# Retention in a two-layer backbone: the seven products of a head's v and g in another order, with their sums of weights built another way

## The chip, the cores and the metric

The kernel runs on one core of a Trainium2 chip. Times are device microseconds (us) of that core. The kernel before ran three times, 1942.5 to 1948.24 us with a median of 1943.03; its profiled execution took 1941.29 us, of which the span from the first to the last instruction is 1939.5. The engines: TensorE (PE, matmuls; PEld is its loading of weights), VectorE (DVE), ScalarE (ACT), GpSimd (POOL) and SyncE (SP). DMA transfers are issued from SP's and POOL's queues.

## The reference, cut to what matters

The model has two layers, on 512 latent and 256 context tokens of width 1024. Layer 0 is attention with spatial gating, layer 1 is retention, and each has a feed-forward block behind it. The change lies in retention, with 8 heads, keys of width 128 and values of width 256:

```
q, k, v, g = jnp.split(h_lat @ w_in, splits, axis=-1)
...
kc, vc = jnp.split(h_ctx @ w_in[:, RET_QK_WIDTH:2 * RET_QK_WIDTH + RET_V_WIDTH], [RET_QK_WIDTH], axis=-1)
...
for d in range(2):
    lg = log_decay[d].astype(jnp.float32)
    rev = (lambda a: a[:, ::-1]) if d == 1 else (lambda a: a)
    s_ctx = retention_final_state(rev(kc), rev(vc), lg)
    outs_lat.append(rev(retention_chunked(rev(q), rev(k), rev(v), lg, s_ctx)))
...
    s = jnp.einsum('bhqd,bhkd->bhqk', qf, kf) * decay_intra
    o = jnp.einsum('bhqk,bhkv->bhqv', s, vf) + jnp.einsum('bhqd,bhdv->bhqv', qf * decay_q, S)
    S = S * decay_chunk + jnp.einsum('bhkd,bhkv->bhdv', kf * decay_k, vf)
...
on = ((o - mu) * lax.rsqrt(var + EPS)).reshape(B, N, RET_V_WIDTH) * gn_g.astype(jnp.float32)
return (jax.nn.silu(g) * on.astype(g.dtype)) @ w_out
```

## The kernel before

Every operand of a matmul is kept as a high and a low part, so a product is three matmuls (`mm3`, L94 to L96; L93 where a sum goes on in an open bank). `split` makes the parts: a copy on ACT (L68) for the high one, a subtraction on DVE (L69) for the low one. A block of weights is loaded raw into one of three buffers (tag `raw`) and split into one of three slots (`slot`), taken in turn.

The kernel is written against a tile scheduler. The code gives an order of emission and named tiles with tags and buffer counts; the scheduler places the instructions on each engine, where they then run strictly in that order, and adds waits where a buffer or a value isn't ready. PSUM has banks by tag: "A" four, "B" two, "C" two.

Retention runs head by head. Head 0 uses plain products and makes, once, sums of the token blocks (`h_sums`). In heads 1 to 7 the projection of the 512 latent tokens to v and g (512 columns a head) is a two-by-two scheme with seven products in place of eight. Each is `product`: 24 matmuls of 128x256, of a block (or sum of blocks) of the tokens with a block (or sum of blocks) of the weights. The blocks of weights are called 11, 12, 21 and 22, and four of the seven operands are sums: t1 = 11+12, t2 = 11+12+22, t3 = 12+22, t4 = 11+12+21+22, as far as signs are folded into the stored weights. The sums are made by DMAs that add into a tile in SBUF (`add`, issued on POOL's queue, 512 KB each).

In the kernel before, one tile (`rwr`) is loaded with 11 and grows to t1, t2 and t4; another (`rwt3`) is loaded with 12 and grows to t3. The products go in the order 11, t1, t2, 21, t3, 22, t4. X, Y and Z are their banks; the sum in X runs over 11, t2, t3 and t4 and is read out between. v and g of the first 256 tokens and the rest are taken from these banks, by copies and subtractions. `nat` is the context's v, in two halves (tile `rn`), which use blocks 11 and 21.

Around the products of head h stand: `rk` and `rq` (keys and queries, 24 matmuls of 128x512 each), the transposes `rt` of head h-1's output and their copies `gt` (`gated`), the transposes `kn` of the keys and their weighted copies `kd` (`k_nat`), eight pieces `wr` of the output projection of head h-1 (`out_steps`, tokens 0 to 3, halves 0 and 1; copies `ypr` on ACT into two buffers, then an adding DMA into the result `yr`, issued on POOL), the scores `rs`, the products `ro` of scores and v (`within`), the states `stc` and `stl` (`states`), whose splits `st` go through `sc` and `cm`, the products `rx` of queries and states (`across`), the context's key `rkc` (`k_ctx`), and the norm on DVE. `bg` steps a background task, the conditioning of a later block: loads `ar`, accumulations `acc`, a few small matmuls `ac`. The output weights of head h, two blocks `rwo` with splits `uwh` and `uwl`, are loaded toward the end of head h and used in head h+1.

In the names of tiles the first digit is the head: `rwt23h` is the high part of t2 in head 3, `rwo31r` the second raw block of output weights of head 3, `wr210` the piece of head 2's output for token block 1, half 0.

Of the kernel before, what the change touches and what calls it, by code (L numbers as in the profile page):

```python
# [8 lines left out]
F32 = mybir.dt.float32  # L9
# [4 lines left out]
ALU = mybir.AluOpType  # L14
AX = mybir.AxisListType

P = 128
D = 1024
# [22 lines left out]
class Trunk:  # L41
# [873 lines left out]
    def retention(self, y, final, gates):  # L915
        S, V, T, G, a = self.S, self.V, self.T, self.G, self.a
        KS = float(np.float32(P) ** np.float32(-0.5))
        with ExitStack() as ctx:
            rp = self.phase(ctx, "retp", 0)
# [132 lines left out]
            def vg_tiles(h):  # L1052
                hd[h]["v"] = [rp.tile([P, 6, 256], F32R, name=f"rv{i}{h}", tag=f"rv{i}", bufs=1) for i in range(2)]
                hd[h]["g"] = rp.tile([P, 4, 256], F32, name=f"rg{h}", tag="rg", bufs=1)

            def score(h, c):
# [162 lines left out]
            def vg_units(h):  # L1219

                d = hd[h]
                u = d["u"] = {}
                src = {"11": vg(h, 0, 0), "12": vg(h, 16, 0), "21": vg(h, 0, 1), "22": vg(h, 16, 1)}
                raws = {}

                def add(t, n):
                    G.dma_start(t, src[n], accum_op=ALU.add)  # L1227

                def raw(n, b):
                    raws[n] = self.bp.tile([P, 1024], F32, name=f"rw{n}{h}r", tag="raw", bufs=3)  # L1230
                    self.load(raws[n], src[b])
# [10 lines left out]
                def b11():  # L1242
                    make("b11", raws["r"])
                    add(raws["r"], "12")

                def t1():
                    make("t1", raws["r"])
                    add(raws["r"], "22")
                    raw("b21", "21")
# [7 lines left out]
                def b21():  # L1257
                    make("b21", raws["b21"])
                    raw("b22", "22")

                return [load, b11, t1, t2, b21] + [
                    lambda n=n: make(n, raws["r" if n == "t4" else n]) for n in ("t3", "b22", "t4")
                ]

            def product(ps, b, w, onto=False):
                for t in range(2):
# [6 lines left out]
            def products(h):  # L1273

                d = hd[h]
                u, v, g = d["u"], d["v"], d["g"]
# [3 lines left out]
                product(X, blk[0, 0], u["b11"])  # L1280
                c11 = self.t2k(f"c11{h}", shape=(P, 2, 256))
                S.copy(c11, X)
                nat(h, [u["b11"], None], 2, "v", range(0, 4))
                yield
                Y = bank("y")
                product(Y, blk["s", 1], u["t1"])
                S.copy(g[:, hi], Y)
# [3 lines left out]
                yield  # L1291
                Z = bank("z")
                product(Z, blk[0, 1], u["b21"])
# [3 lines left out]
                nat(h, [None, u["b21"]], 2, "v", range(4, 8))  # L1297
                yield
                product(X, blk["s", 3], u["t3"], True)
                V.tensor_tensor(out=g[:, hi], in0=g[:, hi], in1=X, op=ALU.subtract)  # L1300
                S.activation(g[:, hi], g[:, hi], AF.Silu)
                yield
                product(Y, blk["s", 4], u["b22"], True)
# [3 lines left out]
                product(X, blk[1, 1], u["t4"], True)  # L1307
                self.split(v[0][:, hi], v[1][:, hi], X)
                yield

            def ahead(h):

                make = vg_units(h)
                make.pop(0)()
                wq = qk(h, 0, "q")
                make.pop(0)()
                return wq, make

            for h in range(8):
                vg_tiles(h)  # L1320
                if h == 0:
                    two = lambda o, n, d0, d1: [
                        w8(self.unit(vg(h, o, i), f"rw{n}{h}{i}", d)) for i, d in enumerate((d0, d1))
                    ]
# [11 lines left out]
                    for half in range(2):  # L1336
# [6 lines left out]
                        for n, f in enumerate(steps):  # L1343
# [29 lines left out]
                    continue  # L1373
                psk = self.ps(f"rk{h}", "A")
# [6 lines left out]
                self.proj_t(psq, wq, 0)  # L1381
                make.pop(0)()
                q_lat(h, psq)
                self.bg()
                f = gated(h - 1)
# [3 lines left out]
                p = products(h)  # L1389
                for n in range(8):  # L1390
                    if make and n > 0:
                        make.pop(0)()
                    next(p, None)
                    o()
                    if n < 2:
                        o()
                    if n == 1:
                        score(h, 0)
                    if n in (1, 3, 4, 5):
                        self.bg()  # L1400
                    if n == 5:
                        within(h, 0)
                        score(h, 1)
                if h < 7:
                    wk = qk(h + 1, 8, "k")
                    k_ctx(h + 1, wk)
                else:
# [5 lines left out]
                    g = rp.tile([P, D], F32, name="g3", tag="s4h", bufs=1)  # L1413
                    self.load(g, gates[0])
                    gates[0] = g
                states(h)
                across(h, 0)
                across(h, 1)
                within(h, 1)
                across(h, 2)  # L1420
                across(h, 3)
                if h < 7:
                    wq, make = ahead(h + 1)
                norm(h)
            self.out_last(o6, lambda: (gated(7), w_out(7)), y, toks, EARLY, final, "r")

# [516 lines left out]
```

## Time and profile before

| what | value |
|---|---|
| median of three runs | 1943.03 us |
| profiled execution / its span | 1941.29 / 1939.5 us |
| granted TensorE clock, mean | 0.976 |
| stage of retention's heads | from about 975 to 1545 us |
| head 3 (1195.3 to 1266.0): length, PE busy | 70.70, 64.11 us |
| head 7 (from 1481.8): longest wait of PE | 2.1 us, `rx` for `st` |
| POOL's adds `rwr`, issue to landing, median | 5.7 us |
| POOL's `yr`, issue to landing, median | 5.6 us |

The page gives the busy time of each engine; a windows view cuts a stretch of time out and gives the same for it, with the granted clock and the share of time that the DMA engines were busy. The waits view names what PE waited for, with the total, the number and the longest. In a timeline row stand the start, the duration, the engine, the line of the code and the operation; the bracket at its end gives how long the engine stood idle before it, and what released it. An issue of a DMA is a row of SPq or POOL; its landing shows as the releaser of the instruction that used the data.

### The profile page before, as it was taken

To read this page: it belongs to the slowest core of one execution; us is meant where nothing else is said; L and a number is where in the kernel's file an instruction comes from. 1 tells how busy PE (TensorE), PEld (TensorE's weight loads), DVE (VectorE), ACT (ScalarE), POOL (GpSimd) and SP (SyncE) were. 2 spreads that over 40 slices of the span, in tenths; PEclk is the share of its full clock that TensorE was granted. 3 is DMA by queue.
4 is the path that set the end of the run, shared out by engine and by line. 5 is a ranking of instruction groups with operands and counts; after the bars stand their busy time and mean duration, and the time that the engine had idled before them with its cause. 6 is when DMAs were issued, how large, how long until landed. Compare 5 with 4: busy or idle time off the path is not lost. (4 is left out here: it accounts for less than half of the span.)

```text
span 1939.5 us, 28779 instructions
## 1 busy us (share of the span) xinstructions
PE 1799.0 (93%) x10760; PEld 1586.0 (82%) x10760; DVE 1432.5 (74%) x2370; ACT 1080.3 (56%) x1947; POOL 417.3 (22%) x540
## 2 busy tenths in 40 slices
PE   8998989979999999999988999899999879999998
PEld 4886767669889899998787978888888769988997
DVE  4844788689887778777788657566555779989887
ACT  6523545666655466555565545445444467667763
POOL 1102213120122222221143132232132010222221
PEclk9999999989999999999999999999999989999999
DMA  8323333142667778776534656855844433877772
GB/s 286 120 86 104 93 112 93 44 142 91 185 158 154 174 147 181 151 158 159 206 125 107 192 108 160 201 115 129 197 91 89 158 111 121 216 201 185 176 168 98
DMA packets 95188, 280.72 MB, mean 145 GB/s; under 512 B 12092, under 2 KB 13628, under 8 KB 95048
## 3 DMA queue, kind: packets, MB, share of 16 engines
q1 hardware_dynamic: 58856, 202.81, 32.5%
q0 software_dynamic: 36192, 76.08, 23.5%
q8 instruction: 84, 1.38, 0.3%
q14 instruction: 56, 0.46, 0.1%
HBM read 209.12 MB, written 52.95 MB: 135 GB/s over the span
## 5 line engine op out<-in xcount | busy, mean ns | idle before, releaser
L216 DVE SCALAR_TENSOR_TENSOR acc<-ar,cs,acc 128x512 f32<-128x512 f32 x256 | 193.5, 774 | 60.8 <-DMA ar<-in_adaw 36.8
L1671 POOL DMA_DIRECT2D yf<-yp x64 | 55.2, 864 | 259.6 <-ACT yp L1667 160.4
L1522 ACT ACTIVATE cv<-pre,cw 128x770 f32<-128x770 f32 (+1 forms) x88 | 80.9, 923 | 27.3 <-DVE pre L1515 26.0
L1523 DVE SCALAR_TENSOR_TENSOR cv<-pre,cw,cv 128x769 f32<-128x769 f32 (+1 forms) x88 | 77.3, 882 | 8.4 <-ACT cv L1522 8.4
L1510 ACT ACTIVATE pre<-px 128x256 f32<-128x256 f32 (+2 forms) x160 | 54.2, 365 | 46.6 <-PE px L93 37.3
L1667 ACT COPY yp<-wf 128x512 f32<-128x512 f32 x118 | 67.8, 576 | 19.3 <-PE wf L96 19.1
L1526 DVE SCALAR_TENSOR_TENSOR cv<-pre,cw,cv 128x769 f32<-128x769 f32 (+1 forms) x88 | 77.3, 882 | 0.7
L1671 POOL DMA_DIRECT2D yd<-ypg x48 | 41.8, 889 | 133.8 <-ACT ypg L1667 132.3
L1671 POOL DMA_DIRECT2D yd<-yp x48 | 42.4, 898 | 127.1 <-ACT yp L1667 126.9
L1179 POOL DMA_DIRECT2D yr<-ypr x40 | 34.6, 865 | 110.2 <-ACT ypr L1175 110.2
L68 ACT ACTIVATE g<-cv 128x770 fp32r<-128x770 f32 (+1 forms) x44 | 32.5, 738 | 31.1 <-DVE cv L1530 31.0
L94 PE MATMUL wr<-uwh,gt 128*128 128x512 f32 x96 | 38.8, 404 | 9.3 <-ACT gt L1137 9.3
L93 PE MATMUL px<-hs,wd 128*128 128x384 f32 x240 | 45.4, 337 | 0.0
L1175 ACT COPY ypr<-wr 128x512 f32<-128x512 f32 x48 | 27.8, 579 | 30.5 <-DMA yr<-ypr 19.7
L1515 DVE TENSOR_TENSOR pre<-pre,pz 128x256 f32<-128x256 f32 (+1 forms) x60 | 20.8, 373 | 32.4 <-PE pz L96 32.4
L93 PEld LDWEIGHTS px<-hs,wd 128*128 128x128 f32 x240 | 42.3, 188 | 1.8 <-DVE pre L1515 0.3
L1510 ACT ACTIVATE pre<-py 128x384 f32<-128x384 f32 (+1 forms) x40 | 17.4, 436 | 45.2 <-DVE cv L1526 27.1
L1227 POOL DMA_DIRECT2D rwr<-in_ret_vg x21 | 18.8, 897 | 108.1 <-DVE rwb111l L69 14.7
L69 DVE TENSOR_TENSOR g<-cv,g 128x770 fp32r<-128x770 f32 (+1 forms) x44 | 36.2, 822 | 7.3 <-ACT g L68 7.2
L1530 DVE TENSOR_TENSOR cv<-cv 128x770 f32<-128x770 f32 (+1 forms) x44 | 36.2, 824 | 4.7 <-ACT cv L1529 3.5
L1529 ACT ACTIVATE cv<-cv 128x770 f32<-128x770 f32 (+1 forms) x44 | 32.7, 743 | 10.7 <-DVE cv L1526 10.6
L95 PE MATMUL wr<-uwl,gt 128*128 128x512 f32 x96 | 38.4, 400 | 0.0
(3424 smaller groups left out, 7237.9 us busy)
## 6 DMA issues: line engine op xcount, KB each, us to landing
ar<-in_adaw SPq DMA_DIRECT2D x96, 512.0 KB
yf<-yp POOLq DMA_DIRECT2D x64, 256.0 KB, 4.6
yd<-yp POOLq DMA_DIRECT2D x54, 256.0 KB, 5.4
yd<-ypg POOLq DMA_DIRECT2D x54, 256.0 KB, 5.1
yr<-ypr POOLq DMA_DIRECT2D x48, 256.0 KB, 5.6
rwr<-in_ret_vg POOLq DMA_DIRECT2D x21, 512.0 KB, 5.7
fin<-xd SPq DMA_DIRECT2D x10, 512.0 KB
xd<-xd SPq DMA_DIRECT2D x8, 512.0 KB
```

The costliest lines, as they stand in the source:

```text
L69: self.V.tensor_tensor(out=lo, in0=src, in1=hi.bitcast(F32), op=ALU.subtract)
L93: mm = lambda *p, **k: self.nc.tensor.matmul(*p, skip_group_check=True, **k)
L94: mm(out, lhs[0], rhs[0], start=first, stop=False)
L95: mm(out, lhs[0], rhs[1], start=False, stop=False)
L216: V.scalar_tensor_tensor(out=acc[s], in0=raw[:, kk * 512 : kk * 512 + 512], scalar=self.cs[:, 8 * s + k : 8 * s + k + 1], in1=acc[s], op0= ...
L1510: S.activation(pre[:, i, c : c + w], ps[:, b : b + w], AF.Copy, scale=scale)
L1522: S.activation(d, s, AF.Identity, scale=w1, bias=b)
L1523: V.scalar_tensor_tensor(out=d[:, 1:W], in0=s[:, 0 : W - 1], scalar=w0, in1=d[:, 1:W], op0=ALU.mult, op1=ALU.add)
L1526: V.scalar_tensor_tensor(out=d[:, 0 : W - 1], in0=s[:, 1:W], scalar=w2, in1=d[:, 0 : W - 1], op0=ALU.mult, op1=ALU.add)
L1530: V.tensor_tensor(out=cv[:, 0], in0=cv[:, 0], in1=cv[:, 1], op=ALU.mult)
L1667: S.copy(v, ps)
L1671: G.dma_start((yd[t] if first else y[t])[:, o], v, accum_op=ALU.add)
```

## The change

The products of heads 1 to 7 go in the order 11, t2, t3, t4, 21, t1, 22. The sum in X thus runs through without other products between, and t1 (after the first `within` and the second score) and 22 (after the states, ahead of the second `within`) stand among the state's steps. The order of emission is written out in place of the loop.

The sums: one tile is loaded with 12 and gets 22 in the head in front (t3), then 11 (t2), then 21 (t4), each after the split of the sum before. t1 is made in another tile, 11 plus 12, in the memory of the v tile (tag `rv1`), which is allocated afterwards. 11, 21 and 22 are also loaded raw as operands of their own. A head has five loads and four adds for them, where it had four and four; each moves 512 KB. Blocks that were called `rwb11`, `rwb21` and `rwb22` when split are now called `rw11`, `rw21`, `rw22`.

The context's bank `rn` is moved from tag "A" to "C" for heads above 0. The background step ahead of `h_sums` in head 0 is taken out, so that each later step of that task comes earlier or later by one in its list. `across` now follows the second `within` for all four token blocks, and `k_ctx` of the next head comes behind it. Some lines of the diff are left out here:

```diff
-                    hd[h]["rn", tp] = self.ps(f"rn{h}{tp}{dst}", "A", (P, 2, 256))
+                    hd[h]["rn", tp] = self.ps(f"rn{h}{tp}{dst}", "C" if h and tp == 2 else "A", (P, 2, 256))
...
-                def load():
+                def start():
                     raws["r"] = rp.tile([P, 1024], F32, name=f"rwr{h}", tag="vgr", bufs=1)
-                    self.load(raws["r"], src["11"])
...
+                    self.load(raws["r"], src["12"])
+                    add("r", "22")
+
+                def first():
+                    plain("11")
+                    raws["t1"] = rp.tile([P, 1536], F32, name=f"rwt1{h}r", tag="rv1", bufs=1)[:, :1024]
+                    self.load(raws["t1"], src["11"])
+
+                def t3():
+                    make("t3", raws["r"])
+                    add("r", "11")
 
                 def t2():
-                    raw("t3", "12")
                     make("t2", raws["r"])
-                    add(raws["r"], "21")
-                    add(raws["t3"], "22")
...
+                    add("r", "21")
+
+                def t4():
+                    make("t4", raws["r"])
+                    add("t1", "12")
...
-                    self.bg(2)
                     sums = h_sums()
...
+                make = hd[h]["make"]
                 psk = self.ps(f"rk{h}", "A")
                 self.proj_t(psk, wk, 0)
                 k_lat(h, psk)
                 psq = self.ps(f"rq{h}", "A")
                 decay(h)
+                make["t3"]()
+                self.proj_t(psq, wq, 0)
+                q_lat(h, psq)
                 if h < 7:
                     wo = w_out(h - 1)
...
+                make["t2"]()
+                f = gated(h - 1)
+                g_tile(h)
+                p = products(h)
+                next(p)
                 self.bg()
...
                 k_nat(h)
+                make["t4"]()
                 pieces = out_steps(h - 1, f, wo) if h < 7 else []
                 o = lambda: pieces and pieces.pop(0)()
...
+                o()
+                o()
+                next(p)
+                o()
+                score(h, 0)
+                make["21"]()
+                next(p)
+                self.bg()
+                o()
+                make["t1"]()
+                v_tiles(h)
+                next(p)
+                if h < 7:
+                    hd[h + 1]["make"] = vg_units(h + 1)
+                    hd[h + 1]["make"]["start"]()
+                o()
+                make["22"]()
+                next(p)
+                self.bg(2)
+                o()
+                next(p)
+                o()
+                o()
                 if h < 7:
                     wk = qk(h + 1, 8, "k")
...
+                within(h, 0)
+                self.bg()
+                score(h, 1)
+                next(p)
+                states(h)
+                next(p)
...
                 within(h, 1)
-                across(h, 2)
-                across(h, 3)
+                for t in range(4):
+                    across(h, t)
                 if h < 7:
-                    wq, make = ahead(h + 1)
+                    k_ctx(h + 1, wk)
+                    wq = ahead(h + 1)
                 norm(h)
```

The scheduler decides what this makes of the order on each engine. On ACT, near the start of head 3, before, from the copies for the queries' rope on (the bracket names what a row waits for: DMASW is a transfer of POOL's queue, DMAHW one of SP's):

```order
L1137 ACTIVATE gt02_11249<-rt20_11251,gng_9014 128x512 [waits PE_49,Activation_49]
L1137 ACTIVATE gt02_11249<-rt21_11258,gng_9014 128x512 [waits PE_49]
L988 ACTIVATE kd03_11265<-kn30_11267,e03_11185 128x256 [waits PE_49,Activation_49]
L988 ACTIVATE kd03_11265<-kn31_11275,e03_11185 128x256 [waits PE_49]
L68 ACTIVATE rwt23h_11355<-rwr3_11106 128x1024 [waits DMASW1_49]
L68 ACTIVATE rq03_11234<-m1q3_11236 128x512 [waits DVE_49]
```

and after the change:

```order
L68 ACTIVATE rwt23h_11240<-rwr3_10794 128x1024 [waits DMASW1_49]
L1139 ACTIVATE gt02_11245<-rt20_11247,gng_9014 128x512 [waits PE_49,Activation_49]
L1139 ACTIVATE gt02_11245<-rt21_11254,gng_9014 128x512 [waits PE_49]
L68 ACTIVATE rq03_11217<-m1q3_11219 128x512 [waits DVE_49]
L1291 COPY c113_11287<-rx3_11262 128x512 [waits PE_49,Pool_49]
L988 ACTIVATE kd03_11318<-kn30_11320,e03_11182 128x256 [waits PE_49]
L988 ACTIVATE kd03_11318<-kn31_11328,e03_11182 128x256 [waits PE_49]
L68 ACTIVATE rwt43h_11336<-rwr3_10794 128x1024 [waits DMASW2_49]
L988 ACTIVATE kd03_11318<-kn30_11320,e13_11184 128x256 [waits DVE_49]
L988 ACTIVATE kd03_11318<-kn31_11328,e13_11184 128x256 [waits DVE_49]
L1177 COPY ypr_9969<-wr200_11341 128x512 [waits DMASW6_49,PE_49]
L1177 COPY ypr_9969<-wr201_11350 128x512 [waits DMASW7_49,PE_49]
```

The split of t2, which waits for an adding transfer, has moved ahead of both `gt`, and the split of t4, which waits for the next one, ahead of the first two `ypr`.

On ACT at the end of head 3, after the change, from the split of the first block of output weights on:

```order
L68 ACTIVATE uwh3_11921<-rwo30r_11923 128x1024 [waits DMAHW3_49]
L68 ACTIVATE rwq4h_11800<-rwq4r_11798 128x1024 [waits DMAHW1_49,PE_49]
L1314 ACT_TABLE_LOAD
L1314 ACTIVATE rg3_11261<-rg3_11261 128x512 [waits DVE_49]
L68 ACTIVATE st03_11696<-stc3_11670 128x2x256 [waits PE_49]
L68 ACTIVATE uwh4_11927<-rwo31r_11929 128x1024 [waits DMAHW4_49]
L1013 COPY sc3_11701<-stc3_11670 128x512 [waits DVE_49]
L68 ACTIVATE rw114h_11806<-rwb114r_11804 128x1024 [waits DMAHW2_49,PE_49]
L1082 COPY of3_11610<-ro31_11733 128x512 [waits PE_49]
L68 ACTIVATE st03_11696<-cm3_11698 128x512 [waits DVE_49]
```

Before, both splits of output weights stood some rows ahead of the state's, with `rwq4h`, a `silu` and others between; now the second stands between the state's first split and the copy `sc`.

The queue of SP issues the loads. Before, around the output weights of head 3:

```order
L54 DMA rwk4r_11689<-in_ret_qk 128x1024 [waits DMAHW3_49,DVE_49]
L54 DMA rwq4r_11799<-in_ret_qk 128x1024 [waits DMAHW4_49,DVE_49]
L54 DMA rwo30r_11884<-in_ret_out 128x1024 [waits DMAHW5_49,DVE_49]
L54 DMA rwr4_11797<-in_ret_vg 128x1024 [waits DMAHW1_49,DMASW2_49,DVE_49]
L54 DMA rwo31r_11890<-in_ret_out 128x1024 [waits DMAHW6_49,DVE_49]
```

and after the change:

```order
L54 DMA rwo30r_11923<-in_ret_out 128x1024 [waits DMAHW6_49,DVE_49]
L54 DMA rwo31r_11929<-in_ret_out 128x1024 [waits DMAHW3_49,DVE_49]
L54 DMA ar171_12007<-in_adaw 128x1024 [waits DMAHW1_49,DVE_49]
L54 DMA rwb214r_12100<-in_ret_vg 128x1024 [waits DMAHW4_49,DVE_49]
L54 DMA rwt14r_11810<-in_ret_vg 128x1024 [waits DMAHW7_49,DMASW0_49,PE_49]
```

The two loads of output weights now stand directly behind each other. The wait for DVE of `rwo30r` is for the low part of `rwk4`, and that of `rwo31r` for the low part of the block `rwo30r` itself, since both go through the three raw buffers.

More of the change, by code (lines that the diff above doesn't have):

```diff
@@ L1224, in vg_units, with add @@
                 raws = {}
[L1226 to L1231, printed above, removed]
+                def add(n, b):
+                    G.dma_start(raws[n], src[b], accum_op=ALU.add)
                 def make(n, src):
@@ L1275, in products @@
                 d = hd[h]
[L1276 removed]
+                u, g = d["u"], d["g"]
                 lo, hi = slice(0, 2), slice(2, 4)
@@ L1279, in products @@
                 X = bank("x")
-                product(X, blk[0, 0], u["b11"])
+                product(X, blk[0, 0], u["11"])
                 c11 = self.t2k(f"c11{h}", shape=(P, 2, 256))
                 S.copy(c11, X)
[L1283 to L1287, printed above, removed]
+                nat(h, [u["11"], None], 2, "v", range(0, 4))
                 yield
@@ L1291, in products @@
                 yield
+                product(X, blk["s", 3], u["t3"], True)
+                S.copy(g[:, hi], X)
+                yield
+                product(X, blk[1, 1], u["t4"], True)
+                v = d["v"]
+                self.split(v[0][:, hi], v[1][:, hi], X)
+                yield
                 Z = bank("z")
-                product(Z, blk[0, 1], u["b21"])
+                product(Z, blk[0, 1], u["21"])
                 V.tensor_tensor(out=c11, in0=c11, in1=Z, op=ALU.add)
@@ L1296, in products @@
                 yield
-                nat(h, [None, u["b21"]], 2, "v", range(4, 8))
+                nat(h, [None, u["21"]], 2, "v", range(4, 8))
                 yield
-                product(X, blk["s", 3], u["t3"], True)
-                V.tensor_tensor(out=g[:, hi], in0=g[:, hi], in1=X, op=ALU.subtract)
+                Y = bank("y")
+                product(Y, blk["s", 1], u["t1"])
+                V.tensor_tensor(out=g[:, hi], in0=Y, in1=g[:, hi], op=ALU.subtract)
                 S.activation(g[:, hi], g[:, hi], AF.Silu)
                 yield
-                product(Y, blk["s", 4], u["b22"], True)
+                product(Y, blk["s", 4], u["22"], True)
                 V.tensor_tensor(out=g[:, lo], in0=Y, in1=g[:, lo], op=ALU.subtract)
@@ L1412, in retention @@
                         self.load(y[t], yd[t])
[L1413 to L1418, printed above, removed]
+                    gg = rp.tile([P, D], F32, name="g3", tag="s4h", bufs=1)
+                    self.load(gg, gates[0])
+                    gates[0] = gg
                 within(h, 1)
-                across(h, 2)
-                across(h, 3)
+                for t in range(4):
+                    across(h, t)
                 if h < 7:
-                    wq, make = ahead(h + 1)
+                    k_ctx(h + 1, wk)
+                    wq = ahead(h + 1)
                 norm(h)
```

67 lines of the change are left out of this document (24 added, 43 removed).

## The prediction, made before the changed kernel was run

> **What bounds the kernel now.** The page comes first, with the waits of TensorE (PE) in the stage of the change, heads 1 to 7.
>
> ```profile
> span 1939.5 us, 28779 instructions
> PE 1799.0 (93%) x10760; PEld 1586.0 (82%) x10760; DVE 1432.5 (74%) x2370; ACT 1080.3 (56%) x1947; POOL 417.3 (22%) x540
> PE rx L94 <- ACT st L68: 16.0, 7, 2.7
> PE rs L94 <- ACT ypr L1175: 12.0, 5, 3.0
> PE wr L94 <- ACT gt L1137: 9.3, 6, 2.2
> ```
>
> PE is the bound, and only its idle time and its clock can change, since the change moves matmuls and drops none. Three waits make 37.3 us over the stage, about 6 us a head: `rx` (the across products) waits for the state's split, `rs` (scores) stands behind output pieces that wait for ScalarE's (ACT) copies `ypr`, and the first output piece waits for the gated output `gt`. If a product stood before each, that would be the most the change could save.
>
> Next, a head is cut out of the windows. I begin one where PE ends `rk`, which frees a weight slot and so starts ACT's next split (for head 3 the 1195.32 row below); call that instant K.
>
> ```profile
> 1056.60:1126.10 69.50, 65.07 (x425) 58.89 (x425) 45.69 (x73) 34.79 (x52) 17.30 (x27) 0.98 0.63 173
> 1126.10:1195.30 69.20, 63.73 (x425) 57.68 (x424) 43.89 (x73) 34.79 (x52) 19.46 (x24) 1.00 0.67 160
> 1195.30:1266.00 70.70, 64.11 (x429) 57.93 (x428) 43.88 (x75) 35.22 (x53) 19.10 (x23) 1.00 0.65 149
> ...
> 1409.60:1481.80 72.20, 65.74 (x430) 59.20 (x429) 36.28 (x63) 33.64 (x51) 18.52 (x22) 0.98 0.53 103
> ```
>
> Columns: length, busy time of PE, PEld, DVE, ACT and POOL, granted clock, DMA share, GB/s. The six heads between 1056.6 and 1481.8 take 70.9 us each on the mean. At clock 1.00 PE is busy 63.7 to 64.1, at 0.98 65.1 to 65.7: there 1 to 2 us of a head goes to the clock.
>
> **The change, waits first.** For PE's lengths, two neighbouring matmuls give the pitch:
>
> ```profile
> 1320.01 0.28 PE L95 MATMUL rkc<-h1c,rwk5h 128*128 128x256 f32 x1
> 1320.13 0.28 PE L96 MATMUL rkc<-h0c,rwk5l 128*128 128x256 f32 x1
> ```
>
> Over a run of such rows it is 0.118 us at 256 columns. So 24 of them (a product, a half of `rn`, `rkc`) take 2.85 us, 12 (`ro`, `stc`, `stl`) 1.42; by columns a piece `wr` takes 1.4 and `rq` 5.6.
>
> *The two adds at a head's start.* The sums come by adding DMAs on POOL's queue, each of which needs the split of the sum before it.
>
> ```profile
> 1195.32 1.06 ACT L68 ACTIVATE rwt13h<-rwr 128x1024 fp32r<-128x1024 f32 x1 [2.83 <-PE rk L95]
> 1200.49 0.93 POOL L1227 DMA_DIRECT2D rwr<-in_ret_vg  x1
> 1203.19 1.27 ACT L1137 ACTIVATE gt<-rt,gng 128x512 fp32r<-128x512 f32 x2
> 1206.38 1.06 ACT L68 ACTIVATE rwt23h<-rwr 128x1024 fp32r<-128x1024 f32 x1 [1.11 <-DMA rwr<-in_ret_vg]
> 1211.14 0.88 POOL L1227 DMA_DIRECT2D rwr<-in_ret_vg  x1 [6.62 <-DVE rwt23l L69]
> rwr<-in_ret_vg POOLq DMA_DIRECT2D x21, 512.0 KB, 5.7
> ```
>
> From K to the second split are 11.06 us here. `gt` runs at K+7.9, ahead of it. In the new order `rwt23h` stands ahead of both `gt` on ACT: its end is K+12.1, the first `gt` then ends at K+12.8 and VectorE's (DVE) remainder at K+13.5. PE comes to the second `kn` at K+12.3 (5.6 `rq`, 0.95 transposes, 2.85, 2.85), and its bank waits for that remainder: **1.25 us**. The next add is issued at K+12.1+1.2 (DVE's split)+0.5 = K+13.8 and lands 5.7 later, at K+19.5; its split `rwt43h` now stands ahead of two `kd` and of `ypr200`, so `ypr200` ends at 19.5+1.06+0.8+0.6 = K+22. PE has done `kn`, two pieces and the t2 product at about K+20, and the third piece waits for that copy's buffer: **1.9 us**. In place of 9.3/6 = 1.6 for `gt` these are 3.15.
>
> *Pieces and scores.* The third copy waits for the first `yr` transfer.
>
> ```profile
> 1212.79 0.87 POOL L1179 DMA_DIRECT2D yr<-ypr  x1 [0.77 <-ACT ypr L1175]
> 1220.22 0.58 ACT L1175 COPY ypr<-wr 128x512 f32<-128x512 f32 x1 [2.77 <-DMA yr<-ypr]
> yr<-ypr POOLq DMA_DIRECT2D x48, 256.0 KB, 5.6
> ```
>
> That took 7.4 us here, with a 512 KB add just ahead in the queue, as it stands after the change too; the median is 5.6. Between that copy's issue and the fourth piece PE now has a piece, a score (0.71) and the t3 product, some 4.3 us of cover in all after ACT's hand-over. The wait is 1.3 by the median, 3.1 by the row; I take **1.95**, nearer the median, since the 512 KB add is further ahead than in the row. The t4 product then waits for ACT's copy of X (the tile is read out between two products): about **0.7**, the copy's 0.58 with its hand-over. Both replace 12.0/5 = 2.4 for `rs`.
>
> *The across products.* In the present order the two loads of output weights overlap:
>
> ```profile
> 1237.29 0.33 SPq L54 DMA_DIRECT2D rwo30r<-in_ret_out  x1
> 1240.96 0.33 SPq L54 DMA_DIRECT2D rwo31r<-in_ret_out  x1
> 1239.71 1.23 DVE L69 TENSOR_TENSOR rwk4l<-rwk4r,rwk4h 128x1024 fp32r<-128x1024 f32 x1
> 1244.66 1.06 ACT L68 ACTIVATE uwh<-rwo30r 128x1024 fp32r<-128x1024 f32 x1 [2.08 <-DMA rwo30r<-in_ret_out]
> 1246.98 1.06 ACT L68 ACTIVATE uwh<-rwo31r 128x1024 fp32r<-128x1024 f32 x1 [0.74 <-DMA rwo31r<-in_ret_out]
> 1249.34 0.33 SPq L54 DMA_DIRECT2D ar<-in_adaw  x1
> 1253.19 1.54 DVE L216 SCALAR_TENSOR_TENSOR acc<-ar,cs,acc 128x512 f32<-128x512 f32 x2 [0.99 <-DMA ar<-in_adaw]
> 1253.37 0.60 ACT L68 ACTIVATE st<-stc 128x512 fp32r<-128x512 f32 x1 [2.15 <-PE stl L95]
> 1255.36 0.59 ACT L1013 COPY sc<-stc 128x512 f32<-128x512 f32 x1 [1.40 <-DVE st L69]
> 1255.98 0.87 DVE L1015 SCALAR_TENSOR_TENSOR cm<-sc,e,stl 128x256 f32<-128x256 f32 x2 [0.65 <-ACT sc L1013]
> 1257.57 1.19 PE L94 MATMUL rx<-st,rq 128*128 128x512 f32 x4 [2.71 <-ACT st L68]
> ```
>
> `rwo31r` goes out as `rwk4l` ends (1240.94): three raw buffers make loads wait for splits. After the change `rwo30r` waits for `rwk4l`, and `rwo31r` for the split of `rwo30r`; on ACT the split of `rwo31r` stands between `st<-stc` and the copy `sc`, which the second half of the state needs. So from the end of the second `rn` half, with a load lasting L: its split and that of `rwk4` 2.9, L, two splits 2.3, hand-over 0.2, L, then split 1.06, `sc` 0.55, `cm` 0.87, `st` 0.6 and hand-overs, 3.2. That makes 8.6+2L. In the same time PE has two pieces, `ro`, a score, t1, `stc`, `stl`, 22 and `ro`: 2.8+1.42+0.71+2.85+2.85+2.85+1.42 = 14.9. The wait is 2L−6.3. L was 3.85 (`ar`), 6.0 (`rwo31r`) and 7.4 (`rwo30r`), the long ones with other loads in flight: waits of 1.4, 5.7 and 8.5. I take L = 4.6, nearer the short one because these two loads go one at a time: **2.8**, in place of 16.0/7 = 2.3. Without the two loads the state's chain (4.2 us from 1253.37 to 1257.57, a little more from `stl`) would be hidden by 22 and `ro`, 4.3 us: the wait would be near 0.
>
> The sum is 1.25+1.9+1.95+0.7+2.8 = 8.6 a head against 6.0: **+2.6**.
>
> *The clock.* Waits of this length can cost more than themselves:
>
> ```profile
> 1327.87 1.62 PE L94 MATMUL rx<-st,rq 128*128 128x512 f32 x4 [2.50 <-ACT st L68]
> 1329.29 0.63 PE L95 MATMUL rx<-st,rq 128*128 128x512 f32 x1
> 1328.00:1332.00 4.00, 4.00 (x11) 3.15 (x12) 1.79 (x4) 1.11 (x1) 0.00 (x0) 0.57 0.93 193
> 1258.00:1262.00 4.00, 4.00 (x19) 3.27 (x18) 2.98 (x8) 1.01 (x2) 0.00 (x0) 1.00 0.94 204
> ```
>
> After a 2.50 us wait the clock fell to 0.57 for four microseconds (1.7 us lost); after the 2.71 us wait at 1257.57 it stayed at 1.00. With five waits a head where three stood I add **0.6** a head; bounds 0 and 1.7.
>
> The Trainium skill ("TensorE: Matmul & The Clock Gate", section "Part 1: The HAM clock gate") halves the clock after at least one wholly idle window of about 3.4 us, the windows running free. By this rule no wait of the sum would cost clock, and the estimate would be smaller by the 0.6 a head, 3 us in all; the trace differs, for its clock fell after 2.50 us, and the measurement decides.
>
> *Heads 1 to 5:* 5 × 3.2 = **+16**. *Head 6:* its `wo` loads come later than the state, so no split stands ahead of `sc`; it gains the 2.3 of `rx` and pays the others: **−0.8** (0 to −2). *Head 7* has no output pieces; on ACT t4's split (end K+20.6) stands ahead of the copy of X that the t3 product needs (end K+21.2), PE is there at K+17.3 (`rq`, transposes, 11, `rn`, `kn` with its wait, t2, a score): 3.9, less the rx wait of 2.1 that is then covered: **+2** (0 to +4). *Head 0* loses a background step, accumulations on DVE ahead of the rope of k:
>
> ```profile
> 1016.85 1.78 DVE L216 SCALAR_TENSOR_TENSOR acc<-ar,cs,acc 128x512 f32<-128x512 f32 x1
> 1019.76 0.74 DVE L216 SCALAR_TENSOR_TENSOR acc<-ar,cs,acc 128x512 f32<-128x512 f32 x1
> 1026.14 0.44 PE L985 MATMUL kn<-ident,m1k 128*128 128x128 f32 x2 [2.29 <-DVE m1k L956]
> 1030.27 0.58 PE L94 MATMUL rs<-rq,rk 128*128 128x256 f32 x1 [3.36 <-ACT rq L68]
> ```
>
> The two waits are 5.65 us, with DVE in one unbroken row. A group of head sums moves ahead of the rope in exchange, and the accumulations come back in head 1, so I take half: **−3** (0 to −5.7).
>
> The added load of 512 KB a head (seven in all) goes out ahead of need, at a DMA share of 0.65: nothing on the path by itself; if it stretched each of the two serial loads by the 0.4 us that a tenth of L makes, it would cost 0.8 a head. Splits and copies on ACT are as many as before.
>
> Sum: 16−0.8+2−3 = **+14**, so 1941.3+14 = 1955.5 for an execution such as the profiled one, whose time is 1.7 under the median shown (1943.0). The forecast is **1957**.
>
> **Rivals.**
>
> *Faster: the covers hold.* If L is at the `ar` row's 3.85 and `yr` at its lowest, about a microsecond under its median, the rx wait is 1.4, that for `ypr210` 0.8, and with half the clock loss a head costs 1.25+1.9+0.8+0.7+1.4 = 6.05, as now: no change. It gets faster when the splits stand no longer where the list has them late, that is, when the adds land before 5.7: at 4.7 the two first waits become 0.25 and 0.9 (`ypr200` comes two microseconds earlier, PE one), and a head costs 0.25+0.9+0.8+0.7+1.4 = 4.05, 1.95 less; with 1 us of clock regained, 5 × 2.95 = 15, and head 0's 3: 1943−18 = **1925**. Against it stands the median of 5.7 in the row of the adds.
>
> *The same:* with the adds at 5.7 but L and `yr` short, the waits only change their names, 6.05 us a head as just worked out; with the ends' −0.8+2−3 that is **1941**.
>
> *Much slower: the loads are as slow as in the trace.* With L at 6.0 the rx wait is 5.7, 3.4 above now, and the clock falls at each (1.7): 5 × (1.15+0.25+3.4+1.7) = 32: **1974**. This has one place, the two loads in series at the end of a head, and decides from L = 4.2 up (there 2L−6.3 is 2.1, the present wait). The `rwo` rows speak for it; that their transfers shared the engines with others speaks against.
>
> *The change doesn't do what it says:* that 22 stands between states and across on PE is certain from the order of instructions; whether `st` is ready behind it isn't, and this is the forecast's case.
>
> **How the numbers follow.** A run of this kernel is told from no change at about 0.3%, 5.8 us. Forecast (1949 to 1966) 0.45, much slower 0.17, the same 0.15, faster 0.23. Slower by over 0.3% takes the first two and a little of the third, **0.63**; same **0.13**; faster **0.24**. The range, leaving out a tenth at each end, is 1925 to 1976; the forecast's own is 1949 to 1966.
>
> **What would show it.** Right: `rx` waits for `st` in heads 1 to 5 by 2 to 4 us with ACT idle for `rwo31r` just before `sc`; `kn` waits for DVE's `gt`; a `wr` waits for `ypr` twice a head; head length 73 to 75 us; the summed waits of PE in the stage above 45 us. Wrong: `rx` without a wait in heads 1 to 5, or a head under 70 us. The time is also wrong if head 0 loses instead of gaining, or if the clock's share moves by more than 2 us a head.

## The result, and the profile after

The changed kernel took 1953.9 us at the median of 7 runs (1951.94 to 1956.96), the kernel before 1943.03 in the 7 runs beside them: a ratio of 1.0050, 95% interval 1.0026 to 1.0075. Measured again with the last experiments it was 1.0053 (1.0033 to 1.0074). The forecast was 1957, slower by 14 us; it is slower by 10 to 11. The profiled execution of the changed kernel took 1956.34 us, 15.1 more than that of the kernel before. Executions of one kernel lie several microseconds apart, so sizes are read from ratios, and the profiles are used for places.

The head of the page, and the waits of PE over heads 1 to 7:

```profile
span 1954.6 us, 28780 instructions
PE 1812.3 (93%) x10760; PEld 1593.8 (82%) x10760; DVE 1432.8 (73%) x2370; ACT 1078.4 (55%) x1947; POOL 413.7 (21%) x540
PE wr L94 <- ACT ypr L1177: 18.7, 11, 2.7
PE kn L985 <- DVE gt L1140: 5.2, 5, 1.7
PE rx L94 <- ACT st L68: 4.8, 6, 0.9
PE rx L93 <- ACT rg L1295: 3.7, 1, 3.7
...
PE rn42v L94 <- ACT rw114h L68: 0.9, 1, 0.9
```

Of the three waits of before, that of `rs` for `ypr` (12.0) and that of `wr` for `gt` (9.3) are gone, and that of `rx` fell from 16.0 to 4.8. In their place pieces wait for `ypr` and `kn` for `gt`. All waits of PE in heads 1 to 7 together are 44.7 us, where they were 42.9: they changed their names and hardly grew. As many instructions of PE as before are busy 13.3 us longer.

Heads 1 to 5, cut at the same instant K as in the prediction:

```profile
1055.20:1127.40 72.20, 66.80 (x426) 60.25 (x425) 44.17 (x73) 34.09 (x52) 18.61 (x27) 0.95 0.60 167
1127.40:1202.00 74.60, 67.34 (x425) 60.28 (x424) 46.62 (x76) 34.24 (x52) 19.02 (x24) 0.95 0.67 156
1202.00:1275.00 73.00, 66.44 (x430) 59.18 (x429) 43.89 (x72) 34.84 (x54) 18.32 (x22) 0.98 0.65 152
1275.00:1348.70 73.70, 66.38 (x429) 59.04 (x428) 46.10 (x76) 34.87 (x53) 17.89 (x22) 0.98 0.66 150
1348.70:1420.70 72.00, 66.42 (x429) 59.15 (x428) 44.21 (x74) 34.91 (x53) 18.40 (x22) 0.98 0.67 154
```

They take 365.5 us in place of 353.0, which is 12.5 of the 15.1. Head 6 (71.6 in place of 72.2) gives 0.6, and what lies ahead of K of head 1 gives 1.4 (1055.2 against 1056.6). From K of head 7 to the end it is 4.6 more, where `rg` at L1295 makes PE wait 3.7.

On ACT in head 4 (K = 1275.0), the start and then the end of the head:

```profile
1285.88 1.06 ACT L68 ACTIVATE rwt24h<-rwr 128x1024 fp32r<-128x1024 f32 x1 [2.70 <-DMA rwr<-in_ret_vg]
1286.84 1.25 ACT L1139 ACTIVATE gt<-rt,gng 128x512 fp32r<-128x512 f32 x2
...
1294.16 1.06 ACT L68 ACTIVATE rwt44h<-rwr 128x1024 fp32r<-128x1024 f32 x1 [4.19 <-DMA rwr<-in_ret_vg]
1295.13 0.82 ACT L988 ACTIVATE kd<-kn,e 128x256 fp32r<-128x256 f32 x2
1295.84 1.07 ACT L1177 COPY ypr<-wr 128x512 f32<-128x512 f32 x2
...
1302.80 0.58 ACT L1177 COPY ypr<-wr 128x512 f32<-128x512 f32 x1 [4.44 <-DMA yr<-ypr]
```

```profile
1329.93 0.58 ACT L68 ACTIVATE st<-stc 128x512 fp32r<-128x512 f32 x1
1332.06 1.06 ACT L68 ACTIVATE uwh<-rwo41r 128x1024 fp32r<-128x1024 f32 x1 [1.56 <-DMA rwo41r<-in_ret_out]
1333.03 0.57 ACT L1013 COPY sc<-stc 128x512 f32<-128x512 f32 x1
1333.49 1.06 ACT L68 ACTIVATE rw115h<-rwb115r 128x1024 fp32r<-128x1024 f32 x1
```

ACT stands idle three times for a transfer while something that PE waits for is behind it in its own queue: 2.70 us ahead of `gt`, 4.19 ahead of the first `ypr`, 1.56 ahead of `sc`. This is how a wait looks that an order makes: idle time on an engine that is 55% busy, and right behind it the copy that the bound engine needs.

### The profile page after: what moved, and what is told of

It reads as the page before. It is cut to its first block, busy times and chain, and to the rows that moved or that the text cites. A ratio compares the mean times of both kernels' runs of the same rounds, so it can differ in the third digit from the quotient of the medians.

```text
span 1954.6 us, 28780 instructions
## 1 busy us (share of the span) xinstructions
PE 1812.3 (93%) x10760; PEld 1593.8 (82%) x10760; DVE 1432.8 (73%) x2370; ACT 1078.4 (55%) x1947; POOL 413.7 (21%) x540
## 5 line engine op out<-in xcount | busy, mean ns | idle before, releaser
L1695 ACT COPY yp<-wf 128x512 f32<-128x512 f32 x118 | 67.8, 577 | 20.7 <-PE wf L96 20.7
L94 PE MATMUL wr<-uwh,gt 128*128 128x512 f32 x96 | 40.9, 426 | 18.7 <-ACT ypr L1177 18.7
L1543 DVE TENSOR_TENSOR pre<-pre,pz 128x256 f32<-128x256 f32 (+1 forms) x60 | 20.8, 371 | 33.0 <-PE pz L96 32.8
L69 DVE TENSOR_TENSOR al<-acc,ah 128x512 fp32r<-128x512 f32 x32 | 22.3, 699 | 23.2 <-ACT ah L68 21.3
L96 PE MATMUL wr<-uwh,gt 128*128 128x512 f32 x96 | 39.1, 407 | 0.0
```

The costliest lines, as they stand in the source:

```text
L69: self.V.tensor_tensor(out=lo, in0=src, in1=hi.bitcast(F32), op=ALU.subtract)
L94: mm(out, lhs[0], rhs[0], start=first, stop=False)
L96: mm(out, lhs[1], rhs[0], start=False, stop=last)
L1695: S.copy(v, ps)
```

## The experiments

Each was timed against the kernel before, in rounds on one chip: e1 to e4 together, e5 to e8, and e9 to e11. The ratio is to that kernel; the changed kernel's own is 1.005.

| kernel | ratio, 95% interval |
|---|---|
| e1, copies first, in part | 1.0028 (1.0012 to 1.0045) |
| e2, output weights early | 1.0009 (0.9988 to 1.0029) |
| e3, 22 before the states | 0.9953 (0.9933 to 0.9973) |
| e4, waits filled with work | 1.0074 (1.0050 to 1.0098) |
| e5, as e3, `rn` under tag A | 1.0091 (1.0066 to 1.0116) |
| e6, e3 and e2 | 0.9949 (0.9928 to 0.9970) |
| e7, e6 and e1 | 0.9910 (0.9887 to 0.9933) |
| e8, t1 and 22 before the steps | 1.0012 (0.9992 to 1.0033) |
| e9, block 11 early | 0.9953 (0.9928 to 0.9979) |
| e10, e7 and e9 | 0.9895 (0.9873 to 0.9917) |
| e11, the changed kernel again | 1.0053 (1.0033 to 1.0074) |

**e1: copies ahead of the splits.**

```diff
-                make["t2"]()
                 f = gated(h - 1)
+                make["t2"]()
...
-                make["t4"]()
...
                 o()
                 o()
                 next(p)
                 o()
+                make["t4"]()
                 score(h, 0)
```

> The changed kernel with gt ahead of the split of t2 on ScalarE, and the split of t4 emitted after three output pieces. Theory (the cost is copies queued behind splits that wait for an add): the kn wait (5.2 us in heads 1 to 6) goes, the waits for ypr (18.7) fall to about 10, the clock falls less often; some 10 to 15 us less than the changed kernel's 1953.9, so 1939 to 1944. Rival (the cost is the added load of 512 KB a head, or the place of the products): no more than 3 us less, 1951 to 1956.

`kn` no longer waits, but the scheduler put t4's split between the first two `ypr`, so the second still stood behind it:

```profile
PE at L261 <- ACT arow L256: 7.7, 4, 2.9
PE rs L94 <- ACT ypr L1177: 7.4, 5, 1.8
...
PE wr L94 <- ACT ypr L1177: 4.2, 2, 2.9
```

The waits for `ypr` fell from 18.7 to 11.6, and a small background matmul (`at`, which needs ACT's `arow`) began to wait. The gain is between the two theories: 0.2%, within the overlap of the intervals. The edit did half of what it was meant to do.

**e2: output weights early.**

```diff
+                if h < 6:
+                    hd[h]["wo"] = w_out(h)
                 if h < 7:
                     wk = qk(h + 1, 8, "k")
```

Head h+1 takes these in place of its own `w_out`.

> The changed kernel with the output weights of head h loaded ahead of the next head's keys, so that no split of them stands amid the state's. Theory (two loads in series delay the state's copy sc): the waits at rn and rx at the end of a head (0.9+0.9 in heads 1 to 5) go to under 0.5 together, with the clock's falls that follow them; 6 to 14 us less, 1940 to 1948. Rival (the wait is the state's own chain): rx waits as before, 1951 to 1956.

The ratio moved by 0.4%, some 8 us, which lies in the theory's 6 to 14; its interval just overlaps that of the changed kernel's first measurement. But the waits that the theory named didn't shrink. `rx` fell to 1.5 us in six, while `rn` of heads 3 to 6 now waits 2.3 to 3.0 each for the split of block 11, one matmul of which the scheduler has ahead of `rx`: at `rn` and `rx` together it is 12.7 us, where it was 9.2. So the end of a head is held by the split of block 11 as well. In this trace `kn` (1.9, was 5.2) and `ry` (0.3, was 2.1) wait less; what made the kernel faster isn't shown.

**e3: 22 before the states.**

```diff
                 score(h, 1)
                 next(p)
-                states(h)
                 next(p)
+                states(h)
```

> The changed kernel with the product 22 emitted ahead of the states, so that only the second within stands between states and across. Theory (22 does cover the state's chain, though not all of it): the wait at rx grows to about 3 us a head, 1.2 to 2 us a head more, 1960 to 1966. Rival (22 covers nothing, since the loads of output weights decide): rx waits as before, 1951 to 1956.

Both theories failed: it is faster, by 1% of the changed kernel's time, and faster than the kernel before. Its waits:

```profile
PE ry L93 <- DVE rg L1313: 12.8, 5, 4.1
...
PE wr L94 <- ACT gt L1139: 5.7, 5, 1.6
PE wr L94 <- ACT ypr L1177: 3.5, 3, 1.4
PE rx L94 <- ACT st L68: 2.1, 1, 2.1
```

The edit moved 22 less than it says, and moved other things too. On PE, 22 still stands behind all of `stc` and the first two matmuls of `stl` in heads 2 to 5, here in head 4 (K = 1276.1):

```profile
1321.93 0.28 PE L95 MATMUL stl<-rv,kd 128*128 128x256 f32 x1
1324.51 0.47 PE L93 MATMUL ry<-rw224h,s4h 128*128 128x256 f32 x1 [2.31 <-DVE rg L1313]
...
1328.98 0.28 PE L96 MATMUL stl<-rv,kd 128*128 128x256 f32 x1
```

Ten matmuls of `stl`, some 1.2 us, changed places with 22. The scheduler also put the next head's whole first half of `rn` ahead of `rx`, so that `rx` is covered all the same, and on ACT the first `ypr` went ahead of t4's split. The waits for `ypr` fell from 18.7 to 3.5.

**e4: the waits filled.**

```diff
+                def fill(ps, n):
+                    for _ in range(n):
+                        T.matmul(ps, f[0][0][:, 0:P], wo[0][0][:, 0:512], start=True, stop=True)
...
                 next(p)
+                if h < 7:
+                    ps = self.ps(f"fill{h}", "C")
+                    fill(ps, 5)
                 o()
...
                 next(p)
+                if h < 7:
+                    fill(ps, 7)
```

> The changed kernel with useless matmuls of 128x512 on TensorE: five ahead of the third output piece (1.2 us by their pitch of 0.233) and seven ahead of the fourth (1.6 us), in heads 1 to 6, 16.8 us of work in all; their results are never read. Theory (idle time of 1.4 to 2.7 us there draws the clock down for 3.4 us afterwards): the waits become work, the clock's falls near 1077, 1157, 1231 and 1451 us vanish, and the time falls by 3 to 7 us, 1947 to 1951. Rival (the falls come by themselves, not from the waits): the time stays or grows by a part of the 16.8 us, 1954 to 1962.

The same stretches around the third and fourth pieces, first of the changed kernel and then with the waits filled (the columns are those of the heads above):

```profile
1075.00:1083.00 8.00, 6.14 (x33) 5.36 (x33) 4.00 (x6) 4.32 (x8) 1.14 (x2) 0.79 0.43 132
1153.00:1161.00 8.00, 6.27 (x32) 5.33 (x31) 2.52 (x3) 3.64 (x6) 4.26 (x6) 0.79 0.98 162
```

```profile
1075.00:1083.00 8.00, 7.79 (x53) 6.87 (x52) 3.27 (x5) 4.20 (x7) 1.14 (x2) 1.00 0.48 95
1153.00:1161.00 8.00, 7.37 (x46) 6.13 (x45) 3.16 (x6) 3.21 (x6) 2.64 (x3) 1.00 0.84 144
```

The clock's falls are gone there, as the theory said: 0.79 became 1.00. So the rival's reason, falls that come by themselves, failed; but the time didn't fall, as the rival said: 1.0074. The waits of the filled kernel:

```profile
PE kn L985 <- DVE gt L1140: 8.8, 6, 1.9
PE ry L93 <- DVE rg L1313: 5.0, 4, 2.6
...
PE wr L94 <- ACT ypr L1177: 2.7, 8, 0.5
```

16 us of waits for `ypr` became work, and 10 us of waits grew elsewhere: 3.6 at `kn`, 2.9 at `ry` (22 behind t1), and 3.6 at `rx`, where t4 waits for the copy of L1298 (4.3, where it was 0.7). This fits a stage in which a PE at full clock comes earlier to the next thing that ACT or DVE hasn't done, so that the price of a fall can't simply be added to that of the wait. What the falls cost alone isn't shown: the fill is 16.8 us of work, and in head 1 the seven matmuls ahead of the fourth piece, 1.6 us, stand where the changed kernel's first trace has no wait.

**e5: the half of `rn` kept away from `rx`.** As e3, with one line more:

```diff
-                    hd[h]["rn", tp] = self.ps(f"rn{h}{tp}{dst}", "C" if h and tp == 2 else "A", (P, 2, 256))
+                    hd[h]["rn", tp] = self.ps(f"rn{h}{tp}{dst}", "A", (P, 2, 256))
```

> As the kernel with 22 ahead of the states, but with the context's bank rn back under tag A, which is full at the end of a head, so that the first half of rn can't stand ahead of rx. Theory (22 behind the states holds its weight slot so long that the next head's block 11 is split too late, and the half of rn that would fill the wait at rx comes only in the next head): without that half ahead of rx the gain of 22 ahead is gone, rx waits 2 to 4 us, and the ratio to the kernel before is 1.003 to 1.010. Rival (the gain came from other orders on ScalarE or from 22 itself): 0.993 to 0.998, as with 22 first alone.

```profile
PE rx L94 <- ACT st L68: 21.7, 7, 3.6
PE wr L94 <- ACT ypr L1177: 10.5, 8, 2.2
```

As the theory said: 1.0091, with `rx` waiting 21.7 in place of 2.1. That is what `rx` costs with neither 22 nor the half of `rn` in front of it. But the order on ACT turned back too (t4's split ahead of the first `ypr` again, 10.5 in place of 3.5), so this run alone can't say which of the two made e3 fast.

**e6 and e7: combinations.** e6 is e3 with the edit of e2, e7 is e6 with the edit of e1.

> 22 ahead of the states, and the output weights loaded ahead of the next head's keys. Theory (with 22 first, 22 waits 2.3 to 4.1 us for DVE's subtraction of t1, which stands behind the split of the first output weights, and that one behind its load): the wait of ry in heads 2 to 5 goes under 1 us, and the ratio to the kernel before is 0.986 to 0.992. Rival (the subtraction is late for another reason): 0.994 to 0.997.

> As the kernel with 22 first and early output weights, with both gt ahead of the split of t2 and the split of t4 emitted after three pieces. Theory (copies behind splits that wait for an add still cost some): the waits of wr for gt and of kn go (1.7 us a head), the ratio to the kernel before is 0.980 to 0.988. Rival (what is won there is waited for at the yr landing further on): the same as without, within 0.3%.

In e6 the wait of `ry` fell from 12.8 to 5.8, so the late subtraction did come from the split of the output weights ahead of it on DVE. The time didn't follow (0.9949 against 0.9953): here the theory's size was wrong, since `wr` and `kn` kept waiting for `gt`, 6.9 and 7.1. In e7 those two waits are gone and the ratio is 0.9910, the theory's direction though less than its size.

**e8: both before the steps.** t1 and 22 go ahead of the first `within`.

```diff
+                next(p)
+                next(p)
                 within(h, 0)
                 self.bg()
                 score(h, 1)
-                next(p)
                 states(h)
-                next(p)
```

> The changed kernel with both t1 and 22 ahead of the first within, so that no product stands amid the state steps; the sums and the rest of the order stay changed. Theory (t1 amid the steps does no harm, 22 does): about as with 22 first, 0.993 to 0.999. Rival (the new sums or the order of the first five products cost the time, not the place of the last two): 1.002 to 1.008.

1.0012 lies between the two and decides neither. `wr` waits 14.2 for `gt` there. It is slower than e3, which has t1 amid the steps, but so much else moved on ACT that the run doesn't show why.

**e9: block 11 early.**

```diff
-                wq = qk(h, 0, "q")
                 make = hd[h]["make"]
                 make["first"]()
+                wq = qk(h, 0, "q")
                 return wq
```

> The changed kernel with block 11 of the next head loaded and split ahead of that head's query weights, so that it takes the slot of t1 and not that of 22; by this order ScalarE also has both gt ahead of the split of t2 and both first ypr ahead of the split of t4. 22 stays amid the state steps, and the first half of rn stays at the start of the next head. Theory (what costs is the half of rn at the start of a head, ahead of the pieces, in place of the end of the head before): the waits for ypr and gt shrink to under 8 us in all, but the ratio to the kernel before stays at 1.000 to 1.004. Rival (the copies behind the splits are the whole loss): 0.992 to 0.997.

The ratio is the rival's: 0.9953, in the same rounds in which the changed kernel (e11) had 1.0053. The products and the state steps have the same order on PE as in the changed kernel. But the half of `rn` doesn't stay wholly at the start of the head, as I had taken for given. At the end of each of heads 1 to 5, 11 of its 24 matmuls stand ahead of `rx`, where the changed kernel has one:

```profile
1331.94 0.28 PE L94 MATMUL rn52v<-rw115h,h0c 128*128 128x256 f32 x1
...
1333.12 0.28 PE L95 MATMUL rn52v<-rw115l,h0c 128*128 128x256 f32 x1
1334.27 1.19 PE L94 MATMUL rx<-st,rq 128*128 128x512 f32 x4 [0.88 <-ACT st L68]
```

So e9 doesn't part the two theories cleanly: it moves the copies, and it moves 1.2 us a head of `rn` in front of `rx`.

> The changed kernel unaltered, on the chip and in the rounds of the two others, so that they can be compared with it directly: 1.003 to 1.008 of the kernel before by either theory.

ACT in head 4 of e9 (K = 1276.1):

```profile
1284.21 1.26 ACT L1139 ACTIVATE gt<-rt,gng 128x512 fp32r<-128x512 f32 x2
...
1290.68 0.59 ACT L1177 COPY ypr<-wr 128x512 f32<-128x512 f32 x1
...
1297.09 1.06 ACT L68 ACTIVATE rwt44h<-rwr 128x1024 fp32r<-128x1024 f32 x1 [4.00 <-DMA rwr<-in_ret_vg]
1298.05 0.57 ACT L1295 COPY rg<-rx 128x512 f32<-128x512 f32 x1
```

`gt` runs at K+8.1 where it ran at K+11.8, the first `ypr` at K+14.6 where it ran at K+20.8. ACT still idles 4.00 us for the add, but what stands behind it now is `rg`, the copy between the products t2 and t3:

```profile
PE rx L93 <- ACT rg L1295: 13.4, 7, 2.3
PE rx L94 <- ACT st L68: 5.4, 6, 1.1
PE wr L94 <- ACT ypr L1177: 3.1, 2, 2.5
```

Of the 18.7 for `ypr` 15.6 went, of the 5.2 for `kn` all, and 0.8 to 1.0 in each of five heads for `rn`; 13.4−3.7 = 9.7 came at `rg`, and smaller waits elsewhere. All waits together are 35.1, against 44.7 in the changed kernel's first trace and 47.5 in e11's, 9.6 to 12.4 less. The medians of the same rounds differ by 20.7 (1953.97 and 1933.31); where the rest of it comes from these waits don't show.

**e10: the combination that beats both.** e7 with the edit of e9.

> 22 ahead of the states, early output weights, and block 11 split ahead of the query weights, with gt and both first ypr ahead of the splits of t2 and t4. Theory (half of rn ahead of rx, copies ahead of splits): as the best so far or better, 0.987 to 0.992 of the kernel before. Rival (the waits that are left come from DVE's subtraction and the yr landings, whatever ScalarE's order): 0.993 to 0.997.

0.9895, in the theory's range: a median of 1925.63 against 1943.71 for the kernel before in the same rounds. `rg` at L1295 is its largest wait, 9.2 us in seven heads.

## Why the prediction was right, point by point

The time was forecast well, and the places of the new waits too. The sizes of the two main terms were not, and that they add up to nearly the right time is in part luck; the paragraph on waits and clock says how.

**The two adds at a head's start: right in mechanism and nearly in size.** `kn` was to wait 1.25 us for `gt`. It waited 5.2/5 = 1.04 in five heads of six, and 8.6/6 = 1.43 in e11's trace of the same kernel. The third piece was to wait 1.9 at K+22 for `ypr` behind t4's split; it waits 1.35 in head 4, at K+21.5. The splits start at K+10.9 and K+19.2 there, forecast K+11.06 and K+19.5. e9 took this order away.

**The `yr` landing: right.** The fourth piece was to wait 1.95; it waits 1.73 to 2.69 in five heads, 2.0 on the mean, and not in head 1. The read-out of X ahead of t4 was put at 0.7 and measured 0.35, and not in every head.

**The two loads in series: seen in the trace, with a smaller wait at `rx`.** In head 4 the two loads lasted 5.2 and 3.65 us from issue to split:

```profile
1320.85 0.33 SPq L54 DMA_DIRECT2D rwo40r<-in_ret_out  x1
1326.07 1.06 ACT L68 ACTIVATE uwh<-rwo40r 128x1024 fp32r<-128x1024 f32 x1 [1.70 <-DMA rwo40r<-in_ret_out]
1328.41 0.33 SPq L54 DMA_DIRECT2D rwo41r<-in_ret_out  x1
```

That is a mean of 4.4 where 4.6 was taken. The wait of 2.8 became 1.04 at `rn` and 0.89 at `rx`, with 0.52 at `ry` ahead of them, 2.45 in all. What was not foreseen is its name: one matmul of the next head's `rn` stands ahead of `rx` and waits for a split that is late by the same idle time on ACT. e2, which takes the loads out of the chain, gave 0.4%, but the waits at `rn` and `rx` didn't shrink there, so that this chain was what held the end of a head isn't shown.

**Waits and clock: the two terms that were mis-sized.** For heads 1 to 5 the forecast was 13 us of added waits and 3 of clock. From the two tables PE is idle 32.1 us there against 28.9 before, 3.2 more, and busy 333.4 against 324.1, 9.3 more. In e11's trace these heads take 10.6 us more than before, 4.2 of it idle and 6.4 busy. The waits were thus put at three to four times what they are: what came for `ypr` and `kn` mostly replaced what went at `rx`, `rs` and `wr`. The busy time came out at two to three times the 3 us, and the two errors partly cancel: 12.5 and 10.6 us where 16 were forecast.

How much of the busy time is the clock stays open. In windows of 2 us the clock falls seven times in these heads, five times in e11's trace and three times before, and a fall loses some 1.7 us: that gives 6.8 of the 9.3 and 3.4 of the 6.4. But the profiled pair stands at mean clocks of 0.971 and 0.976, while over the timed executions of the last rounds the mean is 0.974 both for the changed kernel (12) and for the kernel before (20), with the same 10 us between them. e4 showed besides that taking falls away didn't shorten the time.

**The ends: right in sign.** Head 0 gave 1.4 (forecast 3), head 6 0.6 (0.8); in e11's trace 2.5 and 1.0. In head 7 the wait ahead of t3 is 3.7 where 3.9 was worked out, and the end of the program is later by 4.6, in e11's trace by 1.5 (forecast 2).

**The signs that were named.** `kn` for `gt` and two waits a head for `ypr` were seen, and in head 4 ACT stands idle for the second block of output weights just before `sc`. `rx` waits 0.9 and not 2 to 4; two of the five heads are shorter than 73 us (72.2 and 72.0); and the summed waits, which were to pass 45 us, are 44.7 in one trace and 47.5 in the other.

**The working.** The three waits of before, 2.3, 2.4 and 1.6, add up to 6.3 a head and not to 6.0, which made the forecast 1.5 us longer over five heads. In the much slower rival 1.15 stands where the same terms give 3.15−1.6 = 1.55.

**The added load was no cost that can be seen:** e9 and e10 have all five loads and four adds and are faster than the kernel before. What the load would cost alone wasn't tried.

**The rivals.** The faster one asked for adds that land sooner; they didn't (5.7 us at the median in both pages), but e9 and e10 reach its sign, and e10 nearly its 1925, by another way: fewer copies stand behind those splits. The order around the products, that is the splits, the copies and the place of the half of `rn`, cost 1%. How much of it is the copies alone isn't settled: e1, which moved some of them and left `rn` where it was, gained 0.2%, within the overlap of the intervals. Nor is it shown what the place of 22 is worth. In e3 and e10 it was emitted ahead of the states but stands behind all of `stc` on PE in heads 2 to 5, and only e8, which moved t1 as well, has it ahead of both.

## What to carry to other kernels

When sums of weights are made by adding transfers, ask of each split that ends such a sum what stands behind it on its engine: a split that waits 4 us for a transfer holds every copy behind it, and the bound engine waits for the copies and not for the sum. Read this from the order on the engine that is little busy, not from the products. After a reorder look for the weight slot each block takes, since a swap of two lines, which changes the order in which slots are claimed, was worth 1% here. After an edit that is to move one thing, read from the trace what moved: e3 moved 22 by ten matmuls, and e9 moved part of `rn` unasked. A forecast whose sum comes out right should still be compared term by term, here idle time and busy time. Filling idle time of the bound engine with work tells how free that time is: 16.8 us of it, 0.9% of the kernel, lengthened the time by 0.2% with overlapping intervals, since part of the wait then came elsewhere.

## What the runs showed of the hardware

The clock fell to half for about 3.5 us behind several waits of 1.7 us and more, but not behind each: after the 2.69 us wait that ended at 1230.14 in the changed kernel, not after one of 2.00 that ended at 1376.13; and after two waits of 0.84 and 0.90 with 0.4 us of work between them, which ended at 1407.91:

```profile
1230.00:1234.00 4.00, 3.86 (x14) 3.06 (x15) 2.52 (x3) 3.04 (x6) 2.59 (x4) 0.68 0.95 156
1376.00:1380.00 4.00, 3.52 (x19) 2.82 (x20) 2.52 (x3) 3.04 (x6) 2.59 (x4) 1.00 1.00 181
1409.00:1413.00 4.00, 4.00 (x15) 3.38 (x14) 2.71 (x6) 0.76 (x1) 0.25 (x1) 0.58 0.74 300
```

None of these waits is as long as the idle window of about 3.4 us that the Trainium skill asks for ("TensorE: Matmul & The Clock Gate", section "Part 1: The HAM clock gate"); with the waits for `ypr` filled in e4 the falls behind them went, while falls behind the pair of waits at `rn` and `rx` stayed, at 1119 and 1413 us there. They also differ between executions: in heads 1 to 5 one trace of the changed kernel has seven falls and the other five.
